# Weights split one unit ahead, a head's decay rows loaded at its start, and vector sums moved from GpSimd to VectorE, in a one-core hybrid Fourier/mLSTM transformer layer

## The chip, the core and the metric

One core of one Trainium2 chip runs the whole kernel. The metric is the device time of one launch in microseconds. The profile names the engines PE (TensorE matmul), PEld (its weight loads), DVE (VectorE), ACT (ScalarE), POOL (GpSimd) and SP (SyncE, which here only issues DMA transfers). SBUF is the on-chip memory, PSUM the matmul's accumulators, DRAM the chip's main memory.

## The reference

One layer of a diffusion backbone: 1024 latent tokens and 256 context tokens, width 1024, everything float32. Cut to what is computed:

```python
def half_ffn(h, shift, scale, gate, g_pre, g_post, w13, w2):
    u = modulate(rmsnorm(h, g_pre), shift, scale)
    return h + 0.5 * gate * rmsnorm(swiglu(u, w13, w2), g_post)     # w13: 1024 -> 2*2816, w2: 2816 -> 1024

# token mixing: p = modulate(rmsnorm(h)) @ w_in + b_in, for the latents and for the context
#   xf   512 columns   -> 2-D Fourier transform on the grid
#   q, k, v 1024 each  -> conv + silu on q, k; four heads of 256; mLSTM in both directions
#   o, g_f, g_m        -> sigmoid gates; 16 columns of input and forget gates of the heads
# one direction of the mLSTM, chunk by chunk of 128 tokens:
w   = exp(dmat - m_t)                     # decay between the tokens of a chunk
s   = (q @ k.T) * w
num = a * (q @ C) + s @ v
den = a * (q @ n) + sum(s)
h   = num / max(abs(den), exp(-m_t))
C   = decay * C + (k * wk).T @ v          # the state; the context's last state starts the latents'

h_lat = half_ffn(h_lat, ...a); h_ctx = half_ffn(h_ctx, ...a)
h_lat = h_lat + gate * rmsnorm(merge(fourier, mlstm, o, g_f, g_m) @ w_out)
h_lat = half_ffn(h_lat, ...b)             # the output
```

## The kernel before, in words

**Products.** Every large product is made of float32 operands that are split into a high and a low part; `mm3` (L154) issues three matmuls for one product (high by high, high by low, low by high). So a weight must be split before it can be used: `wunit` (L132) loads a block of 1024 columns into a "wr" tile (DMA at L127 on SP's queue), ScalarE rounds it to the high part "wh" (L141) and VectorE subtracts to get the low part "wl" (L142). wr, wh and wl have three buffers each. Some of the big products (the latents' FFN, q and k, gates, v) are done by Winograd's scheme with seven half-size products in place of eight; their operands are sums of blocks, made on VectorE and GpSimd.

**Order.** A scheduler of the framework places the instructions on the engines' queues; each engine runs its queue in order. The program beside it interleaves: work that has to run beside the products is a generator handed to `later(..., rate=r)`, and each `tick` of a product loop gives it credit (at most 8 are saved up) for as many steps, up to the next `yield`, as the rate says. `drain` runs what is left at once, `defer` puts off a piece by a part of a unit, and `side` is a second such stream.

**Stages**, with the time at which each runs in the trace: start and the first FFN of the latents (`ffn_in`, 0 to 476 us; `wino_out`, 476 to 745); the context's FFN (`ffn_ctx_in`, 44 units of weights, and `ffn_ctx_out`, 22 units of 12 matmuls, 745 to 905), with the residual of the latents, their pre-norm for the mixing (`enter`: two VectorE instructions L423 and L425 and one of ScalarE, L424, for each of 16 tiles) and the sums of the normed tokens for Winograd (`combos`: L1288 on VectorE; L1292 on GpSimd adds high and low parts to whole values, 16 times) beside it; gates and the first Fourier columns (905 to 1012); q, k and gates (`mix_pairs`, 1012 to about 1225); v (`mix_values`, to 1310); the context's projection and states (`ctx_project`, `ctx_states`, 1310 to 1440); the four heads (`mlstm_head`, 1440 to 1830), with gate projections (`feat_major`, four in each head) as the products around them and `ada_rest` as side stream; merge and output projection (1830 to 2060); the second FFN (2060 to 2729).

**v.** `mix_values` keeps for each of 8 pairs the weight sums T2 and T3 in "t" tiles: GpSimd copies T2 out of a loaded block, and makes T3 and the operand of product 4 as differences (L1428, L1433). A finished quarter of v is copied out of PSUM by ScalarE (L1449), and GpSimd adds the bias row (L1450).

**A head.** The latents' 1024 tokens are 8 chunks. For each chunk `rows` (L1549) loads the two rows of decay, 128 columns, over all partitions into one of two "wa" tiles; `weigh` (L1556, L1558) adds the column part and mask on VectorE and takes the exponential on ScalarE; `scores` makes q by k (L1566), weighs it (L1569), q by the state in both directions (L1575), the denominators (L1577 to L1584) and the mixed weights and numerators (L1586 to L1590); `turn` transposes the weights on TensorE (L1596) and copies them back (L1597, ScalarE); `values` multiplies them by v (L1603) and takes the norm (L1604 to L1607); `store` transposes and writes (L1614 to L1620). The order of these steps over the chunks is written out by hand:

```python
for c in range(NCH + 4):
    if 1 < c < NCH + 2: values(c - 2)
    if c < NCH:
        scores(c)
        if c + 1 < NCH: rows(c + 1)
    yield
    if c < NCH - 1: self.state_step(...)          # L1178, L1183
    if 0 < c <= NCH: turn(c - 1)
    yield
    if c > 2 and c < NCH + 3: store(c - 3)
    if c + 1 < NCH: weigh(c + 1)
```

`fetch` issues the loads of the next head's q, k and v one head ahead.

## Time and profile before

| | us |
|---|---|
| median of three launches (2729.97 to 2731.87) | 2731.47 |
| the profiled launch itself | 2731.25 |
| span in that profile, first to last instruction | 2729.5 |
| PE busy in the span | 2623.9 |
| DVE busy | 1949.3 |
| ACT busy | 1165.6 |
| POOL busy | 320.8 |
| mean clock granted to TensorE | 0.985 |

All that the prediction works out is set against the profiled launch, which lies within the three launches' spread; 1.75 us of it lie outside the span. In the windows view, each row is a stretch of the span: its length, then the busy time of each engine with the count of its instructions, then PEclk, the mean clock that TensorE was granted (1.00 is full speed), the share of time that DMA engines were busy and the GB/s they moved. In a row of waits the first name is the engine and line that stood idle, the name behind the arrow what released it, and then come the sum, the count and the longest, in us. In a row of the timeline stand start, duration, engine, line, operation and tiles, and in square brackets the idle time of the engine just before and its releaser.

### The profile page before, as it was taken

To read this page: it belongs to the slowest core of one execution; us is meant where nothing else is said; L and a number is where in the kernel's file an instruction comes from. 1 tells how busy PE (TensorE), PEld (TensorE's weight loads), DVE (VectorE), ACT (ScalarE), POOL (GpSimd) and SP (SyncE) were. 2 spreads that over 40 slices of the span, in tenths; PEclk is the share of its full clock that TensorE was granted. 3 is DMA by queue.
4 is the path that set the end of the run, shared out by engine and by line. 5 is a ranking of instruction groups with operands and counts; after the bars stand their busy time and mean duration, and the time that the engine had idled before them with its cause. 6 is when DMAs were issued, how large, how long until landed. Compare 5 with 4: busy or idle time off the path is not lost. (4 is left out here: it accounts for less than half of the span.)

```text
span 2729.5 us, 34486 instructions
## 1 busy us (share of the span) xinstructions
PE 2623.9 (96%) x11497; PEld 2091.6 (77%) x11497; DVE 1949.3 (71%) x3451; ACT 1165.6 (43%) x2017; POOL 320.8 (12%) x424
## 2 busy tenths in 40 slices
PE   8999999999998899999999999899999999999998
PEld 5778888777776768887777777678887788888876
DVE  5688787899788748856766666555667887865765
ACT  4543333455454435643543443433344433334552
POOL 1111010000003113233000000000001111111000
PEclk9999999999999999999999999999999999999999
DMA  8765454878585542335666554356556654537774
GB/s 286 255 199 172 151 177 158 283 229 273 174 257 189 167 139 89 116 128 160 181 194 211 154 173 120 112 158 195 175 163 198 186 172 156 159 118 258 251 249 140
DMA packets 426266, 499.92 MB, mean 183 GB/s; under 512 B 27329, under 2 KB 262506, under 8 KB 426088
## 3 DMA queue, kind: packets, MB, share of 16 engines
q1 hardware_dynamic: 411016, 451.07, 52.8%
q0 software_dynamic: 14928, 46.59, 4.6%
q8 instruction: 90, 1.47, 0.2%
q14 instruction: 88, 0.72, 0.1%
q10 hardware_dynamic: 144, 0.07, 0.0%
HBM read 387.58 MB, written 110.04 MB: 182 GB/s over the span
## 5 line engine op out<-in xcount | busy, mean ns | idle before, releaser
L154 PE MATMUL mm<-g,wh 128*128 128x512 f32 (+1 forms) x2112 | 689.2, 407 | 6.4 <-DVE m L1931 2.9
L154 PE MATMUL mm<-g,o 128*128 128x512 f32 x2352 | 555.9, 394 | 0.0
L154 PEld LDWEIGHTS mm<-g,o 128*128 128x128 f32 x2352 | 441.7, 188 | 104.0
L154 PEld LDWEIGHTS mm<-g,wh 128*128 128x128 f32 (+1 forms) x2112 | 391.1, 189 | 95.2 <-issue 3.8
L154 PE MATMUL mm<-g,wl 128*128 128x512 f32 (+1 forms) x1056 | 416.8, 396 | 0.2 <-DVE wl L147 0.2
L154 PE MATMUL mm<-wh,g 128*128 128x512 f32 x920 | 295.3, 398 | 4.8 <-ACT wh L141 3.4
L142 DVE TENSOR_TENSOR wl<-wr,wh 128x1024 fp32r<-128x1024 f32 x190 | 233.8, 1233 | 92.6 <-ACT wh L141 92.4
L141 ACT CAST wh<-wr 128x1024 fp32r<-128x1024 f32 x190 | 198.7, 1047 | 210.9 <-PE mm L154 163.5
L154 PE MATMUL mm<-u,wh 128*128 128x512 f32 (+1 forms) x848 | 268.5, 399 | 3.9 <-DVE m L500 2.8
L154 PEld LDWEIGHTS mm<-g,wl 128*128 128x128 f32 (+1 forms) x1056 | 199.1, 189 | 45.2 <-DVE wl L147 0.6
L154 PE MATMUL mm<-wh,u 128*128 128x512 f32 x608 | 205.3, 414 | 5.9 <-ACT t L1449 4.5
L154 PEld LDWEIGHTS mm<-wh,g 128*128 128x128 f32 x920 | 172.6, 188 | 47.5 <-ACT wh L141 4.7
L154 PEld LDWEIGHTS mm<-u,wh 128*128 128x128 f32 (+1 forms) x848 | 159.8, 190 | 41.7 <-DVE m L500 3.2
L154 PE MATMUL mm<-wl,g 128*128 128x512 f32 x460 | 182.8, 397 | 0.2
L154 PE MATMUL mm<-u,wl 128*128 128x512 f32 (+1 forms) x424 | 167.8, 399 | 4.6 <-DVE wl L142 4.6
L610 DVE TENSOR_TENSOR t<-mm,t 128x512 f32<-128x512 f32 x148 | 101.8, 688 | 96.2 <-PE mm L154 96.2
L146 ACT CAST wh<-wr 128x1024 fp32r<-128x1024 f32 (+1 forms) x92 | 81.5, 886 | 165.7 <-PE mm L154 80.1
L154 PEld LDWEIGHTS mm<-wh,u 128*128 128x128 f32 x608 | 119.2, 197 | 33.1 <-ACT t L1449 4.9
L146 ACT CAST o<-wa 128x512 fp32r<-128x512 f32 x108 | 67.0, 621 | 180.0 <-PE mm L154 171.4
L154 PE MATMUL mm<-wl,u 128*128 128x512 f32 x304 | 126.9, 418 | 16.9 <-DVE wl L142 16.8
L328 POOL TENSOR_TENSOR rs_r<-rs_t,mhalf 128x1 f32<-128x1 f32 (+2 forms) x45 | 31.4, 697 | 927.1 <-DVE rs_t L326 822.9
L147 DVE TENSOR_TENSOR g<-t,g 128x512 fp32r<-128x512 f32 x156 | 105.7, 695 | 38.1 <-ACT g L146 30.8
(518 smaller groups left out, 4093.3 us busy)
## 6 DMA issues: line engine op xcount, KB each, us to landing
wr<-in_w_a_dram SPq DMA_DIRECT2D x124, 512.0 KB, 4.3
t<-gx SPq DMA_DIRECT2D x170, 256.0 KB, 4.1
wr<-in_w_in_dram SPq DMA_DIRECT2D x70, 512.0 KB, 3.8
wr<-in_w_b_dram SPq DMA_DIRECT2D x70, 512.0 KB, 4.5
gx<-m POOLq DMA_DIRECT2D x88, 256.0 KB, 3.7
gx<-t POOLq DMA_DIRECT2D x66, 256.0 KB, 4.0
ld<-in_w_ada_dram SPq DMA_DIRECT2D x64, 256.0 KB, 3.0
ld<-h SPq DMA_DIRECT2D x52, 256.0 KB, 3.7
```

The lines of the kernel that those rows point to most:

```text
L141: nc.scalar.copy(hv, rv)
L142: nc.vector.tensor_tensor(lv, rv, hv.bitcast(F32), op=ALU.subtract)
L146: self.nc.scalar.copy(hi, src)
L147: self.nc.vector.tensor_tensor(lo, src, hi.bitcast(F32), op=ALU.subtract)
L154: mul = lambda x, y, start, stop: self.nc.tensor.matmul(out, x, y, start=start, stop=stop, skip_group_check=grown)
L328: nc.gpsimd.tensor_tensor(r, t[:, :n], self.mhalf[:, :n], op=ALU.pow)
L610: add = lambda o, x, y: nc.vector.tensor_tensor(o, x, y, op=ALU.add)
```

## The change

Six things are changed.

- A generator `units()` calls `wunit` for the next block of weights (the context's FFN: for the next two) before it hands out the present one. `ffn_in`, `proj_out`, the context's FFN, `tok_major`, `feat_major`, `merge` and, through `ahead_of`, `mix_values` take their weights from it, and it runs across the loops that follow each other.
- In the context's FFN `combos` adds whole values on VectorE in place of GpSimd, the rates of `enter` and `combos` go from 2.2 and 0.9 to 2.0 and 1.2, and near the end only what `enter` has left is run at once (`until`), not `combos` too.
- In `mix_values` T2 and the first operand of T3 are loaded straight into the "t" tiles, so that the copy falls away; the two differences go from GpSimd to VectorE; and one VectorE addition straight out of PSUM replaces ScalarE's copy and GpSimd's bias addition.
- `gate_rows` of the context lets 12 steps pass in place of 3 before its transposes (L1161).
- In a head the decay rows of all 8 chunks come in 4 transfers of 256 columns at the head's start, into "t" tiles; q is loaded after them and not in `fetch`; weights and weighed scores are written in place.
- In the loop over the chunks `values(c - 2)` stands behind `scores(c)` and the state step, in front of `turn(c - 1)`.

By the counts of instructions VectorE gets 42 more (3389 to 3431), ScalarE 14 fewer, GpSimd 44 fewer (429 to 385), SP 12 fewer; TensorE's matmuls are the same.

```diff
         return hv, lv
+
+    def units(self, srcs, ahead=1):
+
+        held = deque()
+        for src in srcs:
+            held.append(self.wunit(src))
+            if len(held) > ahead:
+                yield held.popleft()
+        yield from held
+
+    def until(self, done):
+
+        while not done():
+            self.flush()
+            try:
+                next(self.bg[0])
+            except StopIteration:
+                self.bg.popleft()
 
...
 
-    def ffn_ctx_out(self, w2, g, late):
-        nc = self.nc
-        w = w2.rearrange("(k p) c -> p k c", p=P)
+    def ffn_ctx_out(self, units, g, late):
+        nc = self.nc
         pd = [[self.mm(), self.mm()], [self.mm(), self.mm()]]
         for k in range(NF):
             if k == NF - 2:
                 late()
-            wh, wl = self.wunit(w[:, k : k + 1, :])
+            wh, wl = next(units)
             self.tick(1)
...
             yield
-        for _ in range(3):
+        for _ in range(3 if full else 12):
             yield
...
                 t = self.s512(tag)
-                nc.gpsimd.tensor_tensor(t, h[k].bitcast(F32), l[k].bitcast(F32), op=ALU.add)
+                tt(t, h[k].bitcast(F32), l[k].bitcast(F32), ALU.add)
                 return t
...
 
+        def held(j, k, h):
+            t = self.s512("t")
+            nc.sync.dma_start(t, w[:, j, k, h * TB : (h + 1) * TB])
+            return t
+
         def weights(n, s):
             hi = self.sb.tile([P, 1024], F32R, tag="wh", bufs=3, name=self.name("wh"))
             lo = self.sb.tile([P, 1024], F32R, tag="wl", bufs=3, name=self.name("wl"))
             cs = [slice(i * TB, (i + 1) * TB) for i in range(2)]
             one = None
             if n == 1:
-                one = raw(0, s, 0)
+                for k in s:
+                    T2[k] = held(0, k, 0)
+            elif n == 6:
+                b12 = raw(0, s, 1)
                 for c, k in zip(cs, s):
-                    T2[k] = self.s512("t")
-                    nc.gpsimd.tensor_copy(T2[k], one[:, c])
-            elif n == 6:
-                b12, b22 = raw(0, s, 1), raw(1, s, 1)
-                for c, k in zip(cs, s):
-                    T3[k] = self.s512("t")
-                    nc.gpsimd.tensor_tensor(T3[k], b22[:, c], b12[:, c], op=SUB)
+                    T3[k] = held(1, k, 1)
+                    tt(T3[k], T3[k], b12[:, c], SUB)
                     tt(T2[k], T3[k], T2[k], ADD)
             elif n == 4:
                 one = raw(1, s, 0)
                 for c, k in zip(cs, s):
-                    nc.gpsimd.tensor_tensor(one[:, c], one[:, c], T2[k], op=SUB)
+                    tt(one[:, c], one[:, c], T2[k], SUB)
             elif n == 5:
...
             t = self.s512(tag)
-            nc.scalar.copy(t, acc[d])
-            nc.gpsimd.tensor_tensor(t, t, br[h], op=ADD)
+            tt(t, acc[d], br[h], ADD)
             return t
...
         keep = {}
-        for n in (1, 6, 7, 4, 5, 3, 2):
+        order = (1, 6, 7, 4, 5, 3, 2)
+        ready = self.ahead_of(lambda x: weights(*x), [(n, s) for n in order for s in steps])
+        for n in order:
             new = n in (1, 5, 2)
             if new:
                 acc = [self.mm() for _ in range(4)]
             for s in steps:
-                T = weights(n, s)
+                T = next(ready)[1]
                 for k, (th, tl) in zip(s, T):
...
         k = [load(8 + 2 * h + i, "u") for i in range(2)]
-        q = [load(2 * h + i, "t") for i in range(2)]
-        return q, k, v
+        return lambda: [load(2 * h + i, "t") for i in range(2)], k, v
 
...
             st.append(t)
+        decay = []
+        for j in range(NCH // 2):
+            decay.append(self.s512("t"))
+            rv = rs.rearrange("(d h) t -> d h t", d=2)[:, h, j * 2 * P : (j + 1) * 2 * P]
+            nc.sync.dma_start(decay[j].rearrange("p (d s) -> p d s", d=2), rv.unsqueeze(0).to_broadcast([P, 2, 2 * P]))
+        q = q()
         ktok = [None] * 4
...
 
-        work, decay = {}, {}
-
-        def rows(c):
-            decay[c] = self.s512("wa")
-            W = decay[c][:, :256].rearrange("p (d s) -> p d s", d=2)
-            rv = rs.rearrange("(d h) t -> d h t", d=2)[:, h, c * P : (c + 1) * P]
-            nc.sync.dma_start(W, rv.unsqueeze(0).to_broadcast([P, 2, P]))
+        work = {}
+        W = lambda c: decay[c // 2].rearrange("p (d s) -> p d s", d=2)[:, :, (c % 2) * P : (c % 2 + 1) * P]
 
         def weigh(c):
 
-            A = decay[c]
-            W = A[:, :256].rearrange("p (d s) -> p d s", d=2)
             for d in range(2):
-                nc.vector.scalar_tensor_tensor(W[:, d, :], W[:, d, :], col(3, c, d), self.mask[:, d, :],
+                nc.vector.scalar_tensor_tensor(W(c)[:, d, :], W(c)[:, d, :], col(3, c, d), self.mask[:, d, :],
                                                op0=ALU.add, op1=ALU.add)
-            nc.scalar.activation(A[:, :256], A[:, :256], AF.Exp)
+            nc.scalar.activation(W(c), W(c), AF.Exp)
 
         def scores(c):
-            A, B = decay.pop(c), self.s512("m")
-            W = A[:, :256].rearrange("p (d s) -> p d s", d=2)
-            SW = A[:, 256:512].rearrange("p (d s) -> p d s", d=2)
+            B, SW = self.s512("m"), W(c)
             S = self.mm()
             for i in range(2):
                 nc.tensor.matmul(S[:, :P], at(q, i, c), at(k, i, c), start=i == 0, stop=i == 1)
             den = self.small([P, 12], "den", bufs=4)
             for d in range(2):
-                nc.vector.scalar_tensor_tensor(SW[:, d, :], S[:, :P], 1.0, W[:, d, :], op0=ALU.mult, op1=ALU.mult,
+                nc.vector.scalar_tensor_tensor(SW[:, d, :], S[:, :P], 1.0, SW[:, d, :], op0=ALU.mult, op1=ALU.mult,
                                                accum_out=den[:, d : d + 1])
...
         for c in range(NCH + 4):
+            if c < NCH:
+                scores(c)
+            yield
+            if c < NCH - 1:
+                self.state_step(kw.pop(c), va(c), db[:, h, c : c + 1], Cf, Cf, self.mm)
             if 1 < c < NCH + 2:
                 values(c - 2)
-            if c < NCH:
-                scores(c)
-                if c + 1 < NCH:
-                    rows(c + 1)
-            yield
-            if c < NCH - 1:
-                self.state_step(kw.pop(c), va(c), db[:, h, c : c + 1], Cf, Cf, self.mm)
             if 0 < c <= NCH:
...
             yield from self.prenorm(self.reload(self.h1, TB, b * TB), r1[b], TB, 0, 1, u2[b])
-        self.later(enter(1), enter(0), rate=2.2)
-        g = self.ffn_ctx_in(w13, *uc)
+            entered.append(b)
+        entered = []
+        self.later(enter(1), enter(0), rate=2.0)
+        units = self.units(self.ctx_units(w13, w2), ahead=2)
+        g = self.ffn_ctx_in(units, *uc)
         gw, U, held = [], {}, []
 
         def late():
-            self.drain()
+            self.until(lambda: len(entered) == 2)
             gw.append(self.gate_weights())
-        self.later(self.combos(u2, U, held), rate=0.9)
-        os, ssq = self.ffn_ctx_out(w2, g, late)
+        self.later(self.combos(u2, U, held), rate=1.2)
+        os, ssq = self.ffn_ctx_out(units, g, late)
 
```

**Where rows move: VectorE in the context's second product.** L142 and L1288 are, in the changed kernel, L142 and L1324; L147 and L165 are the split of a transposed tile. Before, from one unit's split to another:

```order
L142 TENSOR_TENSOR wl_7884<-wr_7881,wh_7883 128x1024
L1288 TENSOR_TENSOR t_7793<-t_7793,ld_7791 128x512
L147 TENSOR_TENSOR u_7801<-ld_7791,u_7800 128x512
L1288 TENSOR_TENSOR t_7808<-ld_7812,t_7808 128x512
L147 TENSOR_TENSOR u_7805<-b_7795,u_7804 128x512
L1288 TENSOR_TENSOR ld_7812<-b_7816,ld_7812 128x512
L1288 TENSOR_TENSOR b_7891<-t_7865,ld_7867 128x512
L1288 TENSOR_TENSOR t_7814<-t_7814,ld_7812 128x512
L147 TENSOR_TENSOR u_7822<-ld_7812,u_7821 128x512
L142 TENSOR_TENSOR wl_7908<-wr_7905,wh_7907 128x1024
```

In the changed kernel, the end of such a stretch (its first five rows stand ahead of these) and the split behind it:

```order
L1324 TENSOR_TENSOR ld_7822<-g_7300,g_7308 128x512
L1324 TENSOR_TENSOR ld_7803<-b_7807,ld_7803 128x512
L1324 TENSOR_TENSOR t_7826<-g_7473,g_7481 128x512
L1324 TENSOR_TENSOR t_7805<-t_7805,ld_7803 128x512
L165 TENSOR_TENSOR u_7813<-ld_7803,u_7812 128x512
L1324 TENSOR_TENSOR b_7828<-t_7820,ld_7822 128x512
L165 TENSOR_TENSOR u_7817<-b_7807,u_7816 128x512
L1324 TENSOR_TENSOR ld_7824<-g_7469,g_7477 128x512
L142 TENSOR_TENSOR wl_7856<-wr_7853,wh_7855 128x1024
```

Before, 8 additions stand between these two splits; now 13, since the sums of high and low parts (operands g and g) are in the same queue.

**TensorE in a head.** The rows from a chunk's `turn` to its `values`, before (L1596 to L1603, tile m_12837; `mm` matmuls of the gate projection cut to the last):

```order
L1596 MATMUL aux_12939<-ident,m_12837 128x128
...
L154 MATMUL mm_12865<-g_7247,wl_12762 128x512
L1603 MATMUL aux_12953<-u_12515,m_12837 128x256
L1566 MATMUL mm_12963<-u_12527,t_12535 128x128
L1566 MATMUL mm_12963<-u_12531,t_12539 128x128
```

In the changed kernel (L1632 to L1639, tile m_12823):

```order
L1632 MATMUL aux_12921<-ident,m_12823 128x128
...
L1602 MATMUL mm_12936<-u_12517,t_12547 128x128
L1602 MATMUL mm_12936<-u_12521,t_12551 128x128
L1611 MATMUL qc_12942<-st_12535,t_12547 128x257
...
L1210 MATMUL mm_12980<-u_12508,kw_12930 128x257
L1639 MATMUL aux_12983<-u_12505,m_12823 128x256
```

`turn` and `values` of a chunk were 7 rows apart and are now 21, with scores and state step of the next chunks between them.

**SP in a head.** Before, each chunk's decay rows (r_l into a "wa" tile) stand between the loads of other streams:

```order
L1549 DMA wa_12860<-r_l 128x2x128
L259 DMA ld_13120<-in_w_ada_dram 128x512
L259 DMA ld_13172<-in_w_ada_dram 128x512
L259 DMA ld_13192<-in_w_ada_dram 128x512
L259 DMA ld_13244<-in_w_ada_dram 128x512
L1549 DMA wa_12925<-r_l 128x2x128
```

In the changed kernel, at the start of the first head:

```order
L1556 DMA t_12539<-r_l 128x2x256
L1556 DMA t_12541<-r_l 128x2x256
L1556 DMA t_12543<-r_l 128x2x256
L1556 DMA t_12545<-r_l 128x2x256
L1535 DMA t_12547<-qk 128x512
L1535 DMA t_12548<-qk 128x512
```

All four transfers of the head stand together, in front of those of q.

More of the change, by code (lines that the diff above doesn't have):

```diff
@@ L710, in ffn_in @@
                     self.put(p, self.gated(p1[1], gate), gx, 1)
+        ready = self.units([w[:, :, c : c + P] for p in range(early, n0) for c in cols(p)])
         for p in range(early, n0):
@@ L846, in wino_out, with proj_units, proj_out @@
                     done(0, 1, d, kept[6][d], acc[d])
-    def proj_out(self, w2, g):
+    def proj_units(self, w2):
         w = w2.rearrange("(k p) c -> p k c", p=P)
         nk = w.shape[1]
+        return [w[:, k0 : min(k0 + 4, nk), dp * 256 : (dp + 1) * 256] for dp in range(ND // 2) for k0 in range(0, nk, 4)]
+    def proj_out(self, w2, g, units):
+        nk = w2.shape[0] // P
         res = []
@@ L892, in residual, with ctx_units, ffn_ctx_in @@
             yield from self.sumsq(o, T, r, name)
-    def ffn_ctx_in(self, w13, uh, ul):
+    def ctx_units(self, w13, w2):
+        w = w13.rearrange("(k p) c -> p k c", p=P)
+        us = []
+        for c in range(6):
+            for k0 in range(0, ND, 2):
+                cols = [h * FF + c * 512 for h in range(2)]
+                wk = w[:, k0 : k0 + 2, :]
+                if c < 5:
+                    us += [wk[:, :, o : o + 512] for o in cols]
+                else:
+                    us.append([wk[:, :, o : o + 256] for o in cols])
+        w = w2.rearrange("(k p) c -> p k c", p=P)
+        return us + [w[:, k : k + 1, :] for k in range(NF)]
+    def ffn_ctx_in(self, units, uh, ul):
         nc = self.nc
-        w = w13.rearrange("(k p) c -> p k c", p=P)
         g = []
@@ L953, in ffn_ctx_out @@
                 late()
-            wh, wl = self.wunit(w[:, k : k + 1, :])
+            wh, wl = next(units)
             self.tick(1)
@@ L1012, in conv, with tok_units, tok_major @@
         nc.vector.scalar_tensor_tensor(out, th, 1.0, t, op0=ALU.add, op1=ALU.mult)
-    def tok_major(self, wcol, stat, ntt, sinks):
+    def tok_units(self, cols):
         w = self.a["w_in"][0].rearrange("(k p) c -> p k c", p=P)
+        return self.units([w[:, k0 : k0 + 2, c : c + 512] for c in cols for k0 in range(0, ND, 2)])
+    def tok_major(self, units, stat, ntt, sinks):
         ps = [self.mm() for _ in range(ntt)]
         for k0 in range(0, ND, 2):
-            ww = self.wunit(w[:, k0 : k0 + 2, wcol : wcol + 512])
+            ww = next(units)
             for kk in range(2):
@@ L1257, in ctx_states, with feat_units, feat_major @@
             yield
-    def feat_major(self, col, u2, sink):
+    def feat_units(self, cols):
         w = self.a["w_in"][0].rearrange("(k p) c -> p k c", p=P)
-        ww = self.wunit(w[:, :, col : col + P])
+        return self.units([w[:, :, c : c + P] for c in cols])
+    def feat_major(self, units, u2, sink):
+        ww = next(units)
         ps = []
@@ L1620, in store @@
             nc.sync.dma_start(dst, hT)
-        rows(0)
         yield
@@ L1787, in merge_in, with merge_units, merge @@
             hm.append((h, l))
-    def merge(self, b, yf, hm):
-        nc, a = self.nc, self.a
+    def merge_units(self):
+        wf = self.a["w_four"][0].rearrange("(k p) c -> p k c", p=P)
+        wm = self.a["w_mproj"][0].rearrange("(k p) c -> p k c", p=P)
+        us = []
+        for d in range(ND):
+            if d % 2 == 0:
+                us.append(wf[:, :, d * P : (d + 2) * P])
+            us.append(wm[:, :, d * P : (d + 1) * P])
+        return us
+    def merge(self, b, yf, hm, units):
+        nc = self.nc
         c0 = b * TB
         y = []
-        wf = a["w_four"][0].rearrange("(k p) c -> p k c", p=P)
-        wm = a["w_mproj"][0].rearrange("(k p) c -> p k c", p=P)
         for d in range(ND):
             if d % 2 == 0:
-                uf = self.wunit(wf[:, :, d * P : (d + 2) * P])
+                uf = next(units)
             pf, pm = self.mm(), self.mm()
@@ L1971, in run @@
         self.z1 = self.scratch([SEQ, 512], "z1")
-        self.fourier_cols(u2, 1)
+        units = self.tok_units([0, 0])
+        self.fourier_cols(u2, 1, units)
         self.drain()
@@ L1977, in run @@
         next(pairs)
-        self.fourier_cols(u2, 0)
+        self.fourier_cols(u2, 0, units)
         self.drain()
@@ L2013, in run @@
             q, k, v = got
-            self.later(self.mlstm_head(h, q, k, v, gates), rate=46.0 / (fills - 0.6 * (h == HEADS - 1)))
-            for i in range(fills):
+            self.later(self.mlstm_head(h, q, k, v, gates), rate=46.0 / (each - 0.6 * (h == HEADS - 1)))
+            for i in range(each):
                 fill()
```

42 lines of the change are left out of this document (19 added, 23 removed).

## The prediction

> **What bounds the kernel now.** I read the page first, then the windows by stage, then what TensorE waits for, then the timeline around the long waits.
>
> ```profile
> PE 2623.9 (96%) x11497; PEld 2091.6 (77%) x11497; DVE 1949.3 (71%) x3451; ACT 1165.6 (43%) x2017; POOL 320.8 (12%) x424
> PE 28%; issue 3%; DMA 3%; DVE 3%; ACT 0%; POOL 0%; DVEq 0%; SPq 0%; POOLq 0%; ACTq 0%
> ```
>
> TensorE is the bound, and the change takes no matmul away. What can be won is its idle time, 2729.5 - 2623.9 = 105.6 us, and the time that it ran at a lower clock. The windows show where these lie:
>
> ```profile
> 142.00:476.00 334.00, 334.00 (x1439) 270.42 (x1438) 267.54 (x416) 119.71 (x201) 37.06 (x66) 1.00 0.54 171
> ...
> 745.00:905.00 160.00, 141.04 (x613) 111.77 (x612) 140.73 (x164) 83.89 (x111) 37.57 (x22) 0.94 0.68 216
> ...
> 1245.00:1310.00 65.00, 60.53 (x266) 49.01 (x265) 38.42 (x46) 26.27 (x36) 15.50 (x19) 0.95 0.61 196
> 1310.00:1440.00 130.00, 124.70 (x557) 95.80 (x556) 89.67 (x243) 59.57 (x105) 10.88 (x49) 0.99 0.63 184
> 1440.00:1830.00 390.00, 360.40 (x1669) 288.42 (x1668) 243.21 (x807) 155.24 (x390) 19.39 (x40) 0.96 0.50 153
> ...
> 2060.00:2160.00 100.00, 96.37 (x412) 77.75 (x411) 83.46 (x116) 52.87 (x80) 20.57 (x15) 0.97 0.67 210
> 2160.00:2650.00 490.00, 489.94 (x2154) 397.46 (x2154) 354.34 (x539) 199.66 (x340) 49.31 (x85) 1.00 0.59 193
> ```
>
> The first row is TensorE at its full pace: 334.00 us over 1439 matmuls, 0.232 us each. In the last row nothing is lost either, so splitting weights earlier is worth nothing there. For the five rows between I take length minus PE busy, plus (1 - PEclk) times length. The context's FFN loses 19.0 + 9.6 = 28.6 us, the end of v 4.5 + 3.3 = 7.7, the context's projection 5.3 + 1.3 = 6.6, the heads 29.6 + 15.6 = 45.2, the start of the second FFN 3.6 + 3.0 = 6.6. Together 94.7 us: no forecast can gain much more, as the change hardly touches the rest. What TensorE waited for, over the whole span:
>
> ```profile
> PE mm L154 <- DVE wl L142: 21.4, 10, 6.6
> PE aux L1603 <- ACT m L1597: 16.0, 10, 2.6
> PE mm L154 <- ACT wh L141: 4.8, 4, 1.4
> PE mm L154 <- ACT t L1449: 4.5, 1, 4.5
> ...
> PE aux L1161 <- ACT m L1143: 3.4, 1, 3.4
> ```
>
> These are the low parts of the weights, a head's turned weights, the first copy of v and the gate transposes: the change touches each of them. The third row stays: three of its four waits fall in the second Fourier product, where `mix_pairs` holds two of the three weight buffers in both kernels.
>
> **The heads.** One turn of the chain, and the wait at its head:
>
> ```profile
> 1519.00 0.36 SPq L1549 DMA_DIRECT2D wa<-r_l  x1
> ...
> 1522.26 0.61 DVE L1556 SCALAR_TENSOR_TENSOR wa<-wa,cols_l,mask 128x128 f32<-128x128 f32 x2 [2.11 <-DMA wa<-r_l]
> ...
> 1526.90 0.47 ACT L1586 ACTIVATE m<-qc,den 128x256 f32<-128x256 f32 x1 [2.84 <-issue]
> ...
> 1527.28 0.26 ACT L1597 COPY m<-aux 128x128 f32<-128x128 f32 x1
> ...
> 1527.59 0.70 PE L1603 MATMUL aux<-u,m 128*128 128x256 f32 x2 [2.46 <-ACT m L1597]
> ```
> ```profile
> DVE wa L1556 <- DMA wa<-r_l: 51.8, 27, 3.8
> DVE acc L268 <- DMA ld<-in_w_ada_dram: 18.7, 20, 2.6
> ```
>
> VectorE stands for 2.11 us until the decay rows land, its queue with scores and denominators moves back by as much, ScalarE's copy L1597 stands behind L1586, which needs the denominators, and TensorE stands 2.46 us at `values`. The change cuts this at both ends. The rows of a whole head are there before the loop, so that most of the 51.8 us falls away; and `values` stands 14 rows later behind `turn`, by the 0.232 us up to 3.2 us (less, since some of these rows are narrower), against a longest stall of 2.6. I let 22 of the 29.6 us idle fall away (L1603's 16.0 and most of the small ones on the same chain), and 7 of the 15.6 of clock.
>
> The new cost is the first decay tile of each head. Some ten rows of TensorE lie between its issue and its use, about 2.3 us, and such loads take longer:
>
> ```profile
> t<-qk SPq DMA_DIRECT2D x16, 256.0 KB, 4.3
> wa<-r_l SPq DMA_DIRECT2D x32, 128.0 KB, 3.7
> ```
>
> So VectorE waits some 2 us once a head, and behind it stand `weigh`, the split of the gate's weights and the first scores. TensorE has gate products in hand there, so I put 0.75 us a head on it, 3 in all. SP issues four loads at once ahead of q's four, 0.36 us each (first row above), so that q and the conditioning weights behind them start 1.5 us later; q has over a hundred rows until its use, and the conditioning loads keep VectorE's second wait of 18.7 us. `values` to `store` shrinks from some 41 rows to 30, still 6 us, for a norm of five short instructions. The heads gain 22 + 7 - 3 = **26 us**. Lower bound: the 16.0 alone, less four stalls as long as the longest, 2.6: 6. Upper bound: 36, all idle time but 3 and 9 of the clock.
>
> **The context's FFN.**
>
> ```profile
> 829.36 0.70 PE L154 MATMUL mm<-wh,u 128*128 128x512 f32 x2
> ...
> 834.31 1.22 DVE L142 TENSOR_TENSOR wl<-wr,wh 128x1024 fp32r<-128x1024 f32 x1
> 835.44 0.74 DVE L425 SCALAR_TENSOR_TENSOR g<-b,ada_l,g 128x512 fp32r<-128x512 f32 x1
> ...
> 835.58 0.79 PE L154 MATMUL mm<-wl,u 128*128 128x512 f32 x1 [4.12 <-DVE wl L142]
> ...
> 837.02 1.05 PE L154 MATMUL mm<-wh,u 128*128 128x512 f32 x2
> ```
> ```profile
> L1292 POOL TENSOR_TENSOR ld<-g,g 128x512 f32<-128x512 f32 x8 | 18.3, 2285 | 45.5 <-PE aux L940 19.2 <-DMA wr<-in_w_a_dram 14.8 <-DVE u L147 6.6
> L1292 POOL TENSOR_TENSOR t<-g,g 128x512 f32<-128x512 f32 x8 | 12.4, 1585 | 0.0
> ...
> L425 DVE SCALAR_TENSOR_TENSOR g<-b,ada_l,g 128x512 fp32r<-128x512 f32 x16 | 14.0, 876 | 0.0
> ...
> L307 DVE SCALAR_TENSOR_TENSOR pre<-ada_l,ca 128x8 f32<-128x8 f32 (+1 forms) x2 | 5.2, 2624 | 0.0
> ...
> L147 DVE TENSOR_TENSOR u<-ld,u 128x512 fp32r<-128x512 f32 x3 | 4.2, 1404 | 0.0
> L610 DVE TENSOR_TENSOR t<-mm,t 128x512 f32<-128x512 f32 x148 | 101.8, 688 | 96.2 <-PE mm L154 96.2
> ```
>
> TensorE waits 4.12 us for a low part that VectorE makes behind pre-norms, and its pairs of matmuls then take 1.05 us in place of 0.70: a stall costs about as much again in clock. But VectorE is here as busy as TensorE, 140.73 against 141.04 us. The 16 whole-value additions bring it 16 x 0.688 = 11.0 us. In return its own instructions run undisturbed: beside GpSimd's additions L425 took 876 ns against 740 (2.2 us over 16), the two L307 took 2624 (nearly all of 5.2 is excess, as 8 columns cannot cost more than L425's 512), L147 1404 against about 690 (2.1 us over three); some 10 us with smaller groups. So VectorE's sum hardly changes, and only its order does: splits two units ahead of use, against 13 additions between two splits. These and the split take 13 x 0.688 + 1.22 = 10.2 us; the unit in work and the two in hand last 3 x 12 x 0.232 = 8.4. One stall of 2 to 5 us with its clock stays there. I take a gain of **6 us**; bounds -5 (the 11.0 us paid in full against the 6) and 15 (half of all that is lost).
>
> The Trainium skill (SBUF — State Buffer, section "SBUF: two separate sides") says that VectorE, when both inputs are in SBUF, and GpSimd take turns on one pair of ports by an exclusive lock, the loser blocked for a whole instruction. This trace agrees as far as GpSimd's additions took 1585 and 2285 ns and VectorE's beside them were longer. By that rule the move pays for itself, as in my sum; without it the stage would be at its lower bound.
>
> **The end of v.**
>
> ```profile
> 1258.77 1.42 DVE L423 SCALAR_TENSOR_TENSOR b<-ld,pre,rb 128x512 f32<-128x512 f32 x2 [1.77 <-DMA ld<-h]
> ...
> 1260.85 2.03 ACT L1449 COPY t<-mm 128x512 f32<-128x512 f32 x4
> ...
> 1261.46 0.79 PE L154 MATMUL mm<-wh,u 128*128 128x512 f32 x1 [4.47 <-ACT t L1449]
> 1261.49 6.80 POOL L1450 TENSOR_TENSOR t<-t,wa 128x512 f32<-128x512 f32 x4 [0.23 <-ACT t L1449]
> ```
>
> ScalarE's copies stand behind a pre-norm that waits for VectorE, which waits for a load. In the change VectorE empties PSUM itself, and it gets 16 bias additions and 8 differences, 24 x 0.688 = 16.5 us, on top of 38.42 in 65. That fits, but the additions can stand behind two pre-norm pairs, 4 x 0.75 = 3 us, and any load they wait for. I let the 4.47 shrink to about 2 and the clock with it: **4 us** gained, from 0 (VectorE as late as ScalarE was) to 7.
>
> **Projection of the context, start of the second FFN.**
>
> ```profile
> 1317.47 0.31 PE L1161 MATMUL aux<-ident,m 36*128 36x36 f32 x2 [3.43 <-ACT m L1143]
> ```
> ```profile
> 2085.55 0.50 PE L154 MATMUL mm<-u,wl 128*128 128x512 f32 x1 [2.25 <-DVE wl L142]
> ```
>
> The first stall lasts 3.43 us; the transposes move some 40 rows of TensorE, about 9 us, later, and their users, the context's states, come well over a hundred rows behind. It goes, with its clock: **4.5 us**, from 2 to 6. The second is one low part late behind the residual's instructions; one unit ahead is 24 matmuls, over 5 us: **4 us**, from 0 to 6. For small stalls that the shifted order makes elsewhere I take 2 off.
>
> **The sum.** 26 + 6 + 4 + 4.5 + 4 - 2 = 42.5 us off the profiled launch of 2731.25, which is 0.2 below the median shown: 2689.
>
> **The rivals.**
>
> - *Only the heads and the transposes gain.* The scheduler had already put splits ahead of use, so `units()` does nothing, and VectorE is the bound in the context's FFN. For it: its 140.73 us, and 489.94 of 490 where splits run without a generator. Against it: the stalls named L142. 2731.25 - 26 - 4.5 = 2701. 20%.
> - *The wait moves on.* In the heads VectorE still stands for conditioning loads (18.7 us) and first decay tiles; heads 10, the rest 8: 2713. 13%.
> - *VectorE becomes the bound, slower.* Its 40 added instructions cost their full 11.0 and 16.5 us where TensorE waits for it. It decides if the groups beside GpSimd do not get shorter: then the first stage needs 140.7 + 11 us on VectorE plus its waits and loses 11 and 5 of clock, v loses 5 and 3. With heads and transposes at 14.5 the sum is 2731.25 + 24 - 14.5 = 2741. 7%.
> - *Nearly all of the 94.7 goes*, all but 20: 2657. 11%.
>
> The forecast keeps 49%. **Range** 2658 to 2716: it takes in the first two rivals and ends at the last. The bounds of the terms added on one side give 6 - 5 + 0 + 2 + 0 - 2 = 1 us gained (2730) and 36 + 15 + 7 + 6 + 6 = 70 (2661); that all fall low together I leave outside. A measurement of this kernel tells about 0.2%, 5.5 us. The third rival is slower, 7%; of the other 93% I put 6 within 0.2%, for low ends that meet; faster by more keeps 87%.
>
> **What would show it.** In the heads' window: PE idle under 10 us, L1556's wait for the decay rows at four waits or so, no L1603 in TensorE's waits. In the context's FFN: GpSimd nearly idle, L425 near 740 ns, one long wait for a low part behind the 13 additions. At the end of v a wait for VectorE's addition in place of ScalarE's copy. No wait at the gate transposes. I am wrong if L1603 still waits, if VectorE's sum in the first stage grows by ten, or if a new wait above 5 us appears outside these five rows.

## The result, and the profile after

The changed kernel takes 2700.29 us, median of four launches (2690.76 to 2704.97); the kernel before, with one launch more, 2730.72. The ratio is 0.9891, 95% interval 0.9857 to 0.9926. The forecast was 2689 with a range of 2658 to 2716: the time lies inside, and 30 us were gained where 42.5 were worked out. Two later measurements beside other kernels gave 0.9866 (0.9848 to 0.9884) and 0.9888 (0.9872 to 0.9904), so the change gains 1.1 to 1.3%.

The profiled launch was the fastest of the four, 2690.76 us. Its engines' row of the page, then its windows, in the prediction's order of stages (in this kernel they begin some 5 to 39 us earlier; each stretch starts and ends near the same matmul as before):

```profile
PE 2607.1 (97%) x11497; PEld 2080.0 (77%) x11497; DVE 1943.2 (72%) x3493; ACT 1157.7 (43%) x2003; POOL 248.7 (9%) x380
```
```profile
740.00:890.00 150.00, 139.83 (x616) 109.84 (x615) 132.21 (x179) 82.47 (x111) 5.17 (x6) 0.97 0.72 229
1230.00:1292.00 62.00, 58.96 (x268) 47.48 (x267) 36.98 (x54) 23.32 (x30) 2.79 (x11) 1.00 0.62 198
1292.00:1420.00 128.00, 123.03 (x553) 93.80 (x552) 87.84 (x237) 58.50 (x102) 10.86 (x49) 1.00 0.64 188
1420.00:1792.00 372.00, 353.47 (x1673) 286.04 (x1672) 246.68 (x816) 158.21 (x393) 20.63 (x40) 0.98 0.54 162
2021.00:2120.00 99.00, 96.11 (x418) 77.43 (x417) 81.91 (x113) 52.45 (x79) 18.55 (x15) 0.98 0.67 216
```

And what TensorE waited for over the span (L172 is the old L154, L1632 and L1633 `turn`, L1650 `store`, L442 the pre-norm on ScalarE, L314 the side stream's):

```profile
PE mm L172 <- DVE wl L142: 8.5, 9, 3.3
PE aux L1650 <- ACT m L1633: 5.0, 3, 2.4
PE aux L1632 <- DVE ada_l L314: 3.9, 1, 3.9
...
PE mm L172 <- ACT g L442: 3.0, 1, 3.0
...
PE qc L1611 <- DVE m L1626: 2.5, 1, 2.5
```

The waits for low parts fell from 21.4 to 8.5 us, and `values` no longer waits for the turned weights. In their place stand `store` and `turn` of the heads, and a pre-norm at the end of v.

By stage, each from the same matmul to the same matmul of TensorE, with the two later profiles of the changed kernel (launches of 2700.55 and 2701.25 us) beside the first:

| stage | before, us | changed, three profiles | gained, mean | forecast |
|---|---|---|---|---|
| context's FFN | 160.1 | 149.5, 149.4, 149.9 | 10.5 | 6 |
| end of v | 65.1 | 61.5, 64.2, 65.1 | 1.5 | 4 |
| projection of the context | 129.9 | 128.8, 130.4, 131.1 | -0.2 | 4.5 |
| four heads | 390.0 | 371.0, 371.4, 371.0 | 18.9 | 26 |
| start of the second FFN | 100.0 | 97.7, 100.3, 99.1 | 1.0 | 4 |
| all else in the launch | | | 2.0 | -2 |
| launch | 2731.25 | 2690.76, 2700.55, 2701.25 | 33.7 | 42.5 |

Two stages carry the gain, the heads and the context's FFN, and in each several edits meet. The experiments take them apart. The three profiles agree better than the stages really do: in runs below that leave a stage as it is in the changed kernel, the heads last 369 to 375 us and the context's FFN 149 to 153, so that 3 us in the heads of one profile tell nothing.

### The profile page after: what moved, and what is told of

It is laid out like the page before. It is cut to its first block, busy times and chain, and to the rows that moved or that the text cites. A ratio compares the mean times of both kernels' runs of the same rounds, so it can differ in the third digit from the quotient of the medians.

```text
span 2689.0 us, 34491 instructions
## 1 busy us (share of the span) xinstructions
PE 2607.1 (97%) x11497; PEld 2080.0 (77%) x11497; DVE 1943.2 (72%) x3493; ACT 1157.7 (43%) x2003; POOL 248.7 (9%) x380
## 4 chain that ended last, share of the span: by engine, by line
PE 74%; DVE 10%; DMA 8%; issue 5%; ACT 2%; SPq 1%; POOL 1%; DVEq 0%; POOLq 0%; ACTq 0%
PE mm L172 66%; DMA ld<-in_w_ada_dram 2%; DMA wr<-in_w_a_dram 2%; PE qc L1611 1%; DVE wl L142 1%; PE mm L1210 1%; DVE u L286 1%; DMA ld<-xT 1%; DMA ld<-h 1%; DVE b L441 1%; DMA t<-r_l 1%; PE aux L1762 1%; ACT wh L141 1%; PE mm L263 1%; DMA ld<-xT_c 0%
## 5 line engine op out<-in xcount | busy, mean ns | idle before, releaser
L172 PE MATMUL mm<-g,wh 128*128 128x512 f32 (+1 forms) x2112 | 686.8, 406 | 4.8 <-DVE m L1972 2.4
L172 PE MATMUL mm<-g,o 128*128 128x512 f32 x2352 | 555.9, 394 | 0.0
L172 PEld LDWEIGHTS mm<-g,o 128*128 128x128 f32 x2352 | 441.8, 188 | 103.9
L172 PEld LDWEIGHTS mm<-g,wh 128*128 128x128 f32 (+1 forms) x2112 | 389.9, 188 | 92.5 <-issue 3.8
L172 PE MATMUL mm<-g,wl 128*128 128x512 f32 (+1 forms) x1056 | 415.9, 395 | 0.0
L142 DVE TENSOR_TENSOR wl<-wr,wh 128x1024 fp32r<-128x1024 f32 x190 | 232.7, 1226 | 95.8 <-ACT wh L141 94.1
L172 PE MATMUL mm<-wh,g 128*128 128x512 f32 x920 | 295.3, 397 | 4.9 <-ACT wh L141 3.4
L172 PE MATMUL mm<-u,wh 128*128 128x512 f32 (+1 forms) x848 | 268.3, 398 | 4.4 <-DVE m L518 2.8
L172 PEld LDWEIGHTS mm<-g,wl 128*128 128x128 f32 (+1 forms) x1056 | 198.6, 188 | 45.0 <-DVE wl L165 0.2
L172 PEld LDWEIGHTS mm<-wh,g 128*128 128x128 f32 x920 | 172.4, 188 | 47.9 <-ACT wh L141 4.7
L172 PE MATMUL mm<-wh,u 128*128 128x512 f32 x608 | 201.9, 406 | 3.9 <-ACT g L442 3.0
L172 PEld LDWEIGHTS mm<-u,wh 128*128 128x128 f32 (+1 forms) x848 | 159.8, 191 | 42.2 <-DVE m L518 3.2
L172 PE MATMUL mm<-wl,g 128*128 128x512 f32 x460 | 182.6, 397 | 0.2
L172 PE MATMUL mm<-u,wl 128*128 128x512 f32 (+1 forms) x424 | 167.8, 398 | 2.5 <-DVE wl L142 2.5
L172 PEld LDWEIGHTS mm<-wh,u 128*128 128x128 f32 x608 | 116.3, 192 | 31.3 <-issue 3.4
L165 DVE TENSOR_TENSOR g<-t,g 128x512 fp32r<-128x512 f32 x156 | 104.5, 687 | 39.2 <-ACT g L164 31.9
L172 PE MATMUL mm<-wl,u 128*128 128x512 f32 x304 | 124.6, 410 | 6.0 <-DVE wl L142 6.0
L164 ACT CAST g<-t 128x512 fp32r<-128x512 f32 x156 | 92.5, 620 | 64.7 <-PE mm L172 46.4
```

What stands on the lines that cost most here:

```text
L142: nc.vector.tensor_tensor(lv, rv, hv.bitcast(F32), op=ALU.subtract)
L164: self.nc.scalar.copy(hi, src)
L165: self.nc.vector.tensor_tensor(lo, src, hi.bitcast(F32), op=ALU.subtract)
L172: mul = lambda x, y, start, stop: self.nc.tensor.matmul(out, x, y, start=start, stop=stop, skip_group_check=grown)
```

## The experiments

Twelve runs of ten kernels (the changed one and one other were run twice) were made in three sets, each set beside the kernel before on one chip. Ratios are to the kernel before of the same set; where two kernels are compared in us, they are of one set or by their ratios.

**The changed kernel again.**

> The changed kernel once more, as the measure for the runs beside it. Its first profile lay 40 us under the kernel before (2690.8 against 2731.3), its median 30 us. If the small gain of the median is scatter of the launches, this run lies 30 to 40 us under the kernel before, and its profile again shows some 11 us gained in the context's FFN and 19 in the heads. If the first profile was a lucky launch, the gain is under 28 us and one of the stages gives it back.

2699.7 us against 2738.5 in this set, ratio 0.9866. The gain is 39 us here, inside the expectation, where the first measurement gave 30 and the third set gives 31. The launches of one kernel within one set lie 3 to 14 us apart; the profile again shows the two gains of the table.

> The changed kernel as the measure for the three runs beside it, in more rounds: 1.1 to 1.4% under the kernel before, as in the two measurements so far.

2699.2 us against 2730.3, ratio 0.9888, as expected.

**The place of `values`.**

```diff
         for c in range(NCH + 4):
+            if 1 < c < NCH + 2:
+                values(c - 2)
             if c < NCH:
                 scores(c)
             yield
             if c < NCH - 1:
                 self.state_step(...)
-            if 1 < c < NCH + 2:
-                values(c - 2)
```

> The changed kernel with values(c - 2) again in front of scores(c), the decay rows still loaded for the whole head. Theory: both ends of the chain mattered, so without the later place TensorE waits again for the turned weights (L1633 in this kernel, L1597 before), a few times for 1 to 2 us: 6 us longer than the changed kernel (3 to 12). Rival: the decay rows alone had made the chain late; then the wait does not return and the time is within 3 us of the changed kernel.

2692.2 us, ratio 0.9839 (0.9818 to 0.9861): 7.5 us shorter than the changed kernel, on the other side of both expectations. So it was run a second time:

> The changed kernel with only the place of values put back, in front of scores, a second time and in more rounds. If the later place costs time, this kernel is again 5 to 9 us shorter than the changed one and its heads last 360 to 364 us against 371 to 375. If the first result was scatter of the launches, the two agree within 3 us.

2690.7 us against 2699.2, ratio 0.9856 (0.9839 to 0.9874): 8.5 us shorter, and none of its five launches is as long as the shortest of the changed kernel. Its heads last 361.5 us in the first profile and 367.0 in the second (360 to 364 were expected), against 371. The later place costs time, of which the second profile shows only some 4 us in the heads. The wait that it was to remove is there again, and the two that replaced it are gone. TensorE's waits in the heads of the later profile:

```profile
PE aux L1639 <- ACT m L1633: 9.6, 6, 3.8
PE mm L1210 <- DVE o L1215: 2.0, 1, 2.0
```

and those of the changed kernel in the same set:

```profile
PE aux L1650 <- ACT m L1633: 5.7, 4, 2.6
PE aux L1632 <- DVE ada_l L314: 4.1, 1, 4.1
PE qc L1611 <- DVE m L1626: 2.5, 1, 2.5
```

**The decay rows.** The changed kernel with `rows`, `weigh` and `scores` of the kernel before, two wa tiles, one load a chunk:

```diff
-        decay = []
-        for j in range(NCH // 2):
-            decay.append(self.s512("t"))
-            ...
+        def rows(c):
+            decay[c] = self.s512("wa")
+            ...
             if c < NCH:
                 scores(c)
+                if c + 1 < NCH:
+                    rows(c + 1)
```

> The changed kernel with the decay rows again loaded one chunk at a time into two wa tiles, values still behind the state step. Theory: VectorE waits again some 50 us for these rows (15.5 in the changed kernel), and the heads take 6 to 14 us longer than in the changed kernel. Rival: the place of values, 14 rows of TensorE or about 3 us later, hides a wait of at most 3.8 us by itself; then the time is within 3 us of the changed kernel or, as the first tile of each head no longer stalls the head's start, up to 4 us shorter.

2705.8 us, ratio 0.9885 (0.9863 to 0.9906), 6.1 us longer than the changed kernel in its set, with intervals that overlap (0.9848 to 0.9884). The theory spoke of the heads, though, and there the run is nearer to the rival: VectorE waits 42.6 us for the rows, and yet the heads last 373.9 us, only 3 more than in the changed kernel, which is within their scatter. So where the rows are late, the later place of `values` seems to help, 390 to 373.9, as if both edits fought the same lateness. The run keeps the splits ahead and the later load of q as well; the splits did nothing for the heads in the run without them (371.4 us), the load of q was not tested alone.

The other way round, the rows alone in the kernel before:

> The kernel before with one part of the change alone: a head's decay rows in four transfers at its start, and q loaded behind them; values stays in front of scores. If the rows carry the gain of the heads, the heads last 360 to 365 us in place of 390 and the kernel is 24 to 30 us shorter than before. If the parts need each other, it gains under 18 us.

2709.0 us against 2730.3, ratio 0.9922 (0.9906 to 0.9938): 21 us, between the two expectations, and the heads last 368.5 us in place of 390.0. The heads of the kernel before, of the changed rows without the later place (this run), and of the later place (with the rest of the change) without the changed rows, as windows of the three profiles:

```profile
1440.00:1830.00 390.00, 360.40 (x1669) 288.42 (x1668) 243.21 (x807) 155.24 (x390) 19.39 (x40) 0.96 0.50 153
```
```profile
1438.00:1806.50 368.50, 350.03 (x1668) 283.59 (x1667) 245.47 (x814) 156.95 (x393) 19.69 (x40) 0.99 0.55 163
```
```profile
1424.70:1798.60 373.90, 350.25 (x1669) 280.83 (x1668) 245.39 (x810) 156.94 (x391) 19.98 (x40) 1.00 0.53 161
```

Rows alone take 21.5 us off the stage, the later place with all but the rows 16, both together 19. So the rows alone give what the heads gained. The 2.5 us between 368.5 and 371 are within the scatter; that the later place gives some back rests on the launches of the two runs above.

**Why the later place costs.** In the changed kernel `values`, `turn` and `store` follow each other within nine rows of TensorE and share two small PSUM buffers with the side stream. One line tests that:

```diff
-            pv = self.aux()
+            pv = self.mm()
             nc.tensor.matmul(pv[:, :DH], B[:, P : 2 * P], va(c)[:, :DH], ...)
```

> The changed kernel with the result of values in one of the four product buffers of PSUM (mm) in place of one of the two small ones (aux); the order of the steps is the changed one. Putting values back in front of scores made the changed kernel about 8 us shorter. Theory: with values directly in front of turn and store, three results in a row want the two aux buffers, which the side stream uses too, and the third waits until VectorE or ScalarE has emptied the first; with values in mm the waits at L1632 and L1650 (together some 10 us in the heads) fall away and the kernel is 5 to 10 us shorter than the changed one. Rival: the norm between values and store has too little time in the later place; then L1650 still waits and the time stays within 3 us of the changed kernel.

2701.4 us, ratio 0.9886 (0.9865 to 0.9908): no gain, and the heads last 374.5 us. TensorE's waits in them, longest sums first:

```profile
PE mm L1639 <- DVE t L1605: 3.6, 1, 3.6
PE mm L1602 <- DVE st L1215: 3.6, 3, 2.7
PE aux L1650 <- DVE m L1643: 3.5, 1, 3.5
```

The waits at L1632 are gone, but as long ones stand elsewhere, all released by VectorE. In the same set a kernel with the heads as changed has 374.6 us, so the stage did not move either way. This does not clear the buffers of PSUM: `values` (L1639) now waits for instructions that read the product buffers (L1605, L1215), so one wait for a buffer has taken the place of another. L1650 now waits for the norm L1643, as the rival said, though for 3.5 us only. Why the later place costs stays open.

**A try at a better version.**

```diff
+        # in fetch(h + 1): the first decay tile of the next head
+        first = self.s512("wa")
+        nc.sync.dma_start(first..., rows of chunks 0 and 1)
         ...
-        ready = self.ahead_of(lambda x: weights(*x), ...)     # v
+        ready = ((x, weights(*x)) for x in ...)
```

together with `values` in front of `scores`:

> The changed kernel with values again in front of scores, the first decay tile of heads 2 to 4 loaded one head ahead into a wa tile, and v's weights not split ahead. Theory: the first is worth 8 us by its own run, the second takes VectorE's waits for decay rows from some 15 us to 4 and with them one stall of 2.5 us and its clock, the third gives back 2 to 3 us at the end of v: 11 us shorter than the changed kernel, about 1.8% under the kernel before. Rival: the load ahead collides with q, k and v of the next head, and the third was scatter; then it is no shorter than the kernel with only the first, 1.6% under the kernel before.

2697.6 us, ratio 0.9881 (0.9861 to 0.9901): no better than the changed kernel. By the ratios it is 7 to 11 us longer than with `values` alone put back, but those runs are of other sets, and its interval overlaps that of the second (0.9839 to 0.9874). VectorE's waits for decay rows in the heads:

```profile
DVE t L1599 <- DMA t<-r_l: 22.6, 9, 3.5
```

They are 13.1 us in 5 waits where `values` alone was put back, and 22.6 in 9 here: the first tile is early, but more of the other loads are late, and I did not follow why. The time is the rival's; that the load collides with q, k and v is not shown. The end of v, 60.5 us, is short in this run, but it is about 60 in two runs with v's weights ahead as well (the decay rows one chunk at a time, the gate transposes), so the third part looks like scatter, as the rival had it.

**The splits ahead.**

```diff
             held.append(self.wunit(src))
-            if len(held) > ahead:
+            if held:
                 yield held.popleft()
```

and the same for v:

> The changed kernel with units() and the generator of v's weights handing out each block as soon as it is asked for, none ahead; all else as changed. Theory: the splits ahead give a part of the 10.6 us gained in the context's FFN and the 2 to 3 us at the start of the second FFN: 8 us longer than the changed kernel (3 to 15), with L142 back among TensorE's longest waits in these two stages. Rival (the first in the prediction): the scheduler had already put the splits ahead of use; then the time is within 3 us of the changed kernel.

2704.4 us, ratio 0.9887 (0.9866 to 0.9907), 4.7 us longer than the changed kernel in its set: inside the theory's 3 to 15, but the intervals overlap (0.9848 to 0.9884). The stages agree with a small effect: the context's FFN takes 154.2 us against 149.4 to 149.9, and TensorE waits there 13.1 us for low parts (L142) against 6.0 to 6.8. The start of the second FFN, 98.9, shows none, and the end of v is shorter in this profile, 58.8 us against 61.5 to 65.1. Its window in this run and in the changed kernel (its third profile):

```profile
1239.30:1298.10 58.80, 58.50 (x265) 47.05 (x264) 36.24 (x52) 23.28 (x30) 2.80 (x11) 1.00 0.61 205
```
```profile
1233.70:1298.80 65.10, 60.70 (x266) 48.92 (x265) 36.78 (x53) 23.32 (x30) 2.79 (x11) 0.95 0.59 188
```

**The additions of `combos`.**

```diff
-                tt(t, h[k].bitcast(F32), l[k].bitcast(F32), ALU.add)
+                nc.gpsimd.tensor_tensor(t, h[k].bitcast(F32), l[k].bitcast(F32), op=ALU.add)
```

> The changed kernel with the 16 whole-value additions of combos back on GpSimd. Theory of the prediction: VectorE gets 11 us of work less, but its instructions beside GpSimd's take longer again (L443 near 870 ns in place of 740), so that the two cancel: the context's FFN takes between 4 us less and 6 us more than in the changed kernel. Rival: the move alone made the gain of 10.6 us there; then the stage is 8 us or more longer. Second rival: VectorE's load alone counts; then it is 5 us or more shorter and the wait behind 13 additions is gone.

2710.0 us, ratio 0.9920 (0.9903 to 0.9938), against 0.9866 to 0.9891 for the changed kernel: 8 to 15 us longer. The stage is some 13 us longer, so the first rival holds. Its 163.4 us are 3 more than in the kernel before: with the additions on GpSimd, the splits two units ahead and the new rates gained nothing here. One of its stalls shows how the additions reach TensorE. A split that takes 1.22 us elsewhere lasts 6.04, until four additions have ended, and TensorE stands 6.79 us for a low part:

```profile
863.98 6.04 DVE L142 TENSOR_TENSOR wl<-wr,wh 128x1024 fp32r<-128x1024 f32 x1
864.02 4.91 POOL L1328 TENSOR_TENSOR t<-g,g 128x512 f32<-128x512 f32 x4
...
870.08 0.79 PE L172 MATMUL mm<-wl,u 128*128 128x512 f32 x1 [6.79 <-DVE wl L142]
```

And the same line alone, the other way round, in the kernel before:

> The kernel before with one line changed: the 16 whole-value additions of combos on VectorE in place of GpSimd, all rates and splits as before. Putting them back on GpSimd cost the changed kernel 10 us in the context's FFN. If that is the work of GpSimd's additions on VectorE's instructions beside them, this kernel is 7 to 11 us shorter than before. If the gain needs the splits two units ahead and the new rates, it gains under 4 us or loses, since 11 us of work come on top of a VectorE that was as busy as TensorE.

2721.1 us against 2730.3, ratio 0.9964 (0.9952 to 0.9976): 9.3 us gained by this one line, with no split ahead and no rate changed. The context's FFN in the kernel before, in this run, in the changed kernel and in the changed kernel with the additions back on GpSimd:

```profile
745.00:905.00 160.00, 141.04 (x613) 111.77 (x612) 140.73 (x164) 83.89 (x111) 37.57 (x22) 0.94 0.68 216
```
```profile
740.30:892.50 152.20, 140.73 (x613) 111.75 (x612) 132.58 (x179) 84.46 (x111) 7.01 (x6) 0.94 0.71 223
```
```profile
743.60:893.50 149.90, 137.95 (x614) 108.24 (x613) 131.88 (x179) 82.50 (x111) 5.17 (x6) 0.98 0.73 229
```
```profile
741.30:904.70 163.40, 141.44 (x613) 111.64 (x612) 137.47 (x165) 83.00 (x111) 32.87 (x22) 0.94 0.67 210
```

The third busy time is VectorE's. In the second row it has the 16 additions, 11.0 us, on top of the work of the first, and is busy 8.2 us less. TensorE's waits for low parts in the four windows are 16.8, 8.4, 6.8 and 16.6 us: they go with the place of the additions.

**The gate transposes.**

```diff
-        for _ in range(3 if full else 12):
+        for _ in range(3):
```

> The changed kernel with 3 in place of 12 steps before the gate transposes of the context. I forecast a gain of 4.5 us for this; the profiles showed about nothing. Theory: the stall of 3.4 us went from the gate transposes to the transposes of the convolved keys (L1248), which wait for the same chain on VectorE and ScalarE; then this kernel shows the 3.4 us at L1193 again, none at L1248, and its time is within 3 us of the changed kernel. Rival: something else in the stage got longer by chance; then this kernel is 4 to 5 us longer than the changed one.

2698.6 us, ratio 0.9887 (0.9867 to 0.9906): no difference to the changed kernel. TensorE's waits in this stage, in the changed kernel and in this run:

```profile
PE aux L1248 <- ACT wa L1240: 1.6, 1, 1.6
...
PE aux L1248 <- DVE u L1251: 1.1, 1, 1.1
```
```profile
PE aux L1193 <- ACT m L1175: 3.4, 1, 3.4
```

The stall of 3.4 us comes back at the gates and the two at L1248 go, as the theory said. The stage lasts 131.3 us here against 128.8 to 131.1.

## Why the prediction was right, and which of its steps were not

**The bound and the sign.** TensorE is the bound, no matmul went, and nearly all of the gain, 31.7 of 33.7 us, is idle time and clock in the five rows named. That the sum came so close is in part luck: four of its terms were together 17 us too high, and the context's FFN gained 4.5 us more than forecast. The time lies near the first rival's 2701, but not for its reason: that rival had nothing gained in the context's FFN.

**The heads: 26 forecast, 18.9 measured.** That the decay rows start the chain is right: VectorE's wait for them went from 51.8 us to some 15 (first profile of the changed kernel), and the rows alone, in the kernel before, take 21.5 us off the stage.

```profile
DVE t L1594 <- DMA t<-r_l: 15.5, 6, 3.6
```

The term that was too large is the idle time: 22 less 3 of the 29.6 us was to go, and "PE idle under 10 us" was to show it; 11 went, and 18.5 are left (372.00 less 353.47). The clock's part, 7, came out about as forecast (15.6 to 7.4). The step that failed is "the change cuts this at both ends". I added the later place of `values` as if it could only help; it gave back 7.5 and 8.5 us in two measurements against the same kernel without it. I had looked at the distance from `turn` to `values` and dismissed the one from `values` to `store`; in the changed kernel TensorE waits at `store` and `turn`, and moving the PSUM buffer out of the way did not help. The price of the first decay tile came out about as forecast for TensorE: one wait of 2.5 us at L1611, where VectorE had stood over 3 us for the tile, against 3 in the sum; VectorE's own waits, six of together 14.7 to 15.5 us, are twice my 8. "The rows of a whole head are there before the loop" holds for the first head alone. In the other three the first tile goes out 4 to 6 us before its use and the other three 12 to 17 us behind it, as in the last head of the first profile:

```profile
1640.43 0.38 SPq L1556 DMA_DIRECT2D t<-r_l  x1
...
1652.88 0.92 SPq L1556 DMA_DIRECT2D t<-r_l  x2
...
1656.49 0.38 SPq L1556 DMA_DIRECT2D t<-r_l  x1
```
```profile
1645.24 0.88 DVE L1594 SCALAR_TENSOR_TENSOR t<-t,cols_l,mask 128x128 f32<-128x128 f32 x3 [3.57 <-DMA t<-r_l]
```

The conditioning loads stayed, 22 to 24 us against 18.7.

**The context's FFN: 6 forecast, 10.5 measured.** The sum for VectorE failed: I let 11.0 us come and some 10 go, so that its load "hardly changes". The groups of the kernel before against those of the run with only the additions moved, where GpSimd makes none of these additions, show that 16 go: 4.9 for the two L307, 4.2 for six splits of transposed tiles (I had counted three), some 3.5 for the fourteen L1288 (I had not priced them at all), 2.2 for L425, 1 for L142; by the whole windows it is 11.0 + 8.2 = 19, of which 1.2 are one split less in the second window. So VectorE fell from 140.7 to 132.6 and was no longer as busy as TensorE. That one line, made alone, takes 7.8 us off the stage (9.3 off the launch). The splits two units ahead and the new rates add 2.3 by the difference of the two middle windows above; the splits are worth 5 by the run without them, and nothing where the additions stay on GpSimd. The wait behind 13 additions, forecast as one of 2 to 5 us, is there:

```profile
875.05 0.65 PE L172 MATMUL mm<-wl,u 128*128 128x512 f32 x1 [3.26 <-DVE wl L142]
```

**The end of v: 4 forecast, 1.5 measured** (0 to 3.6). "Any load they wait for" decided it: in the second profile VectorE stands 4.7 us for a load of h, and the first of its PSUM additions (L1442) and the pre-norm behind that load end just before TensorE goes on:

```profile
1243.82 0.75 DVE L441 SCALAR_TENSOR_TENSOR b<-ld,pre,rb 128x512 f32<-128x512 f32 x1 [4.70 <-DMA ld<-h]
...
1246.95 0.68 DVE L1442 TENSOR_TENSOR t<-mm,wa 128x512 f32<-128x512 f32 x1
1247.06 0.72 ACT L442 ACTIVATE g<-b,ada_l 128x512 fp32r<-128x512 f32 x1 [1.74 <-DVE b L441]
...
1247.78 0.77 PE L172 MATMUL mm<-wh,u 128*128 128x512 f32 x1 [3.31 <-ACT g L442]
```

4.47 became 3.0, 3.3 and 4.4 in the three profiles, where I had said about 2. In the eleven profiles with the new way of emptying PSUM, TensorE's stall follows VectorE's longest wait for a load of h: 0.3 to 1.4 us where that is 1.2 to 2.0, 1.8 and 2.0 where it is 3.5 and 3.8, 3.0 to 4.4 where it is 4.3 to 5.6. The short ones come with v's weights ahead and without.

**The projection: 4.5 forecast, nothing measured.** The step "it goes, with its clock" was wrong. The gate stall did go, but I did not say what is late next: the transposes of the convolved keys wait 1.6 and 1.1 us in its stead. I had taken one stall less for so much less time in the stage.

**The start of the second FFN: 4 forecast, 1.0 measured.** The wait of 2.25 us for a low part shrank to 1.2 to 1.5. "One unit ahead" did not remove it, and a wait that the kernel before does not have here, for a sum of squares that VectorE adds up (L382), takes 0.6, 2.5 and 1.9 us in the three profiles.

**The rivals.** "The wait moves on" is partly right, in the heads and in the projection. "VectorE becomes the bound" is refuted where it was placed: the groups beside GpSimd did get shorter. That the generator does nothing is nearly right for all but the context's FFN.

## What to carry to other kernels

Two edits against the same lateness need not add: price the second on the kernel that already has the first, and look at what the moved step comes closer to. Work moved from GpSimd to VectorE can make VectorE's load smaller, so sum up what every group of VectorE loses beside GpSimd before calling VectorE full. The best version here is the changed kernel without the moved `values`: 0.9839 and 0.9856 of the kernel before, some 8 us under the changed one.

## What the runs showed of the hardware

An instruction of VectorE on 4 columns of 128 rows took as long as four additions of GpSimd beside it (kernel before, timeline of both engines):

```profile
850.63 5.08 DVE L307 SCALAR_TENSOR_TENSOR pre<-ada_l,ca 128x4 f32<-128x4 f32 x1
850.67 5.01 POOL L1292 TENSOR_TENSOR t<-g,g 128x512 f32<-128x512 f32 x4
```

With the additions on VectorE the same instruction took 0.16 us, and an addition 0.69 us in place of GpSimd's 1.59 and 2.29 (means of its two groups). The weight split of 6.04 us beside four additions, in the run with the additions back on GpSimd, is a second case. This is what the Trainium skill (SBUF — State Buffer, section "SBUF: two separate sides") describes as an exclusive lock, where the loser is blocked for a whole instruction; in these two cases the loser was blocked until four in a row had ended. A group's mean hides this: of the 16 L425 in the kernel before, two ran beside an addition and took 1.79 us each, and 14 took 0.75. L423, 16 times in the same stage and unchanged at 749 ns, says nothing about it, as none of the 16 ran while an addition did.

Launches of one kernel differ by up to 14 us (2690.76 to 2704.97 for the changed one), and between profiles the stages that the change does not touch differ too: 266, 269 and 269 us in the three profiles for the second product of the first FFN. A gain of 4 us in one stage cannot be read from one profile.
